# Two-layer fp32 encoder: the modulation sums are copied out one filling step ahead of their transposes, and GpSimd sums all squares of the first layer's last norm for two ranges

## The chip, the cores and the metric

The kernel runs on one core of a Trainium2 chip. The metric is the device time of one launch in microseconds (us). The kernel before takes 1818.6 us, the median of three runs (1816.88, 1818.6 and 1819.7 us).

## The reference

A small encoder of two layers with d = 1024 works on two sequences, a prompt of 256 tokens and a sample of 512 tokens, in fp32. Each sequence has a condition vector c, from which each layer makes six modulation vectors:

```python
for l in range(DEPTH):
    mod = jax.nn.silu(c) @ adaln_w[l] + adaln_b[l]
    sh1, sc1, g1, sh2, sc2, g2 = [t[:, None, :] for t in jnp.split(mod, 6, axis=-1)]
    h = rmsnorm(x, norm_g[l, 0]) * (1 + sc1) + sh1
    y = mlstm_mixer(...) if l % 2 == 0 else swa_mixer(...)
    x = x + g1 * y
    h = rmsnorm(x, norm_g[l, 1]) * (1 + sc2) + sh2
    x = x + g2 * conv_ffn(h, ...)
return rmsnorm(x, final_g)
```

Layer 0 mixes with an mLSTM of four heads, run forward and backward, whose output is multiplied by a sigmoid gate of its own and projected. Layer 1 mixes with attention in a sliding window. Both have a feed-forward part with a convolution of width 3 over the tokens (d_ff = 2816). The norm is `y = xf * lax.rsqrt(jnp.mean(xf * xf, axis=-1, keepdims=True) + EPS)`, then times its gain.

## The kernel before

**Layout.** Activations lie transposed: 128 channels on the partitions, tokens along the free axis, eight chunks of channels for the 1024. There are 768 tokens: the sample's 512 come first in the order of work, in two ranges of 256, and the prompt's 256 are the third range (`RANGES`). A product in fp32 is made of three matmuls: each operand is split into a high and a low half (`whi`, `wlo` for weights, `zh`, `zl` for normed activations), and high times high, high times low and low times high are summed. The split of a weight block of 128x1024 is a cast on ScalarE (ACT, L278) and a subtraction on VectorE (DVE, L279), after its DMA from HBM through SyncE's queue (SP).

**Order of the work.** The code is written as one stream per engine with tiles in rotating buffers; a scheduler then decides the order of instructions on each engine from the order of the code and its own estimate of when things are ready. On the chip each engine runs its own stream in that order and waits at an instruction until its inputs and its buffer are there, so nothing behind a waiting instruction passes it.

**Filling steps.** The modulation of layer 0 for the groups 2 to 5 (a group is 1024 columns of adaln_w: g1, sh2, sc2, g2) is made inside the mLSTM, in pieces. `adaln_g` (from L472) is a generator: it fetches two blocks of adaln_w (`raw`), yields, multiplies them with silu(c) on TensorE (PE; rows `ps<-raw,silc`, four matmuls of 32 output rows for a block, into four column groups of one bank `ps`), and so on through eight blocks. At the end the sums in `ps` are copied into `sb` (one half by DVE at L499, the other by ACT at L500), PE transposes the two halves (L503), and DVE adds the bias into `mod` (L508). Four such generators are chained as `self.fillp` (L1761). Heads 1 to 3 of the mLSTM take 11 steps each from the chain: after a piece of q and k (L790), after every second tile of v (L805), and two at each sequence (L872). What is left of the chain after the heads and the output gate is run at once by `first` (L1764).

```python
self.fillp = chain(*(self.adaln_g(0, grp) for grp in range(2, 6)))
self.fill = self.adaln_v(1, pool)
act = self.mlstm(pool, gates, xt)
for _ in chain(self.fillp, self.fill):
    pass
```

A second generator, `adaln_v`, makes layer 1's modulation on DVE (L540, rows `ada<-raw,silc,ada`) and sums over partitions with ones on PE; its steps (`self.fill`) are taken between those of `fillp`.

**The end of the mLSTM.** After head 3 come the output gate's products (`ps<-zh,whi` and so on, 128x256 and 128x512): ACT takes the sigmoid (`sg`, L916), POOL (GpSimd) multiplies it with the mLSTM's output (L917), and ACT and DVE split the result (`slab<-sg`, L278 and L279). Then the output projection starts, with `ps<-slab,whi` 128x384 as its first row.

**The norms.** `Norm` (L91) sums the squares of the eight channel chunks of a range. ACT squares a chunk (L112). With `on_pe` = n, all chunks but the last n are added up on POOL (L121), one after another, and the sum and the n last squares are each multiplied by a constant matrix (`inv`) on PE for each 128 tokens, summed over the channels (`pa<-inv,nt`, 128x2). DVE adds epsilon (L161), POOL raises to the power -1/2 (L162), and PE spreads the factor `nr` over the partitions (`pa<-kct,nr`). DVE multiplies it with x (L583), ACT adds the shift and rounds into `zh` (L585), and DVE makes `zl` (L586). In `down` the last pass of a layer's feed-forward part makes the tiles of x (`pa` or `ps<-slab,whi` and `wlo`, added to x by DVE at L624) and squares them at once for the norm that follows; `keep` is given in layer 0 alone. In layer 0 these norms have `on_pe` = 2: five adds on POOL and six products with inv in each range. The first window products of layer 1 (`ps<-zh,whi`, `ps<-zl,whi`, `ps<-zh,wlo`) follow the second range's zh and zl while the tiles of the next range are still made.

Of the kernel before, what the change touches and what calls it, by code (L numbers as in the profile page):

```python
# [24 lines left out]
RANGES = ((256, 512, 0), (512, 768, 0), PROMPT)  # L25
# [55 lines left out]
def col(t):  # L81

    return t + (GAP if t >= 256 else 0)
# [101 lines left out]
class Net:  # L185
# [290 lines left out]
    def adaln_g(self, l, grp):  # L476

        nc = self.nc
        fetch = lambda k: self.raw(
            self.io["adaln_w"][l, k * P : (k + 1) * P, grp * 1024 : (grp + 1) * 1024]  # L480
        )
        part = [fetch(0), fetch(1)]
        yield
        ps = self.ps()
        for k in range(0, KC, 2):

            with self.tc.manual_schedule(engines={mybir.EngineType.PE}):
                for z in (1, 0):
                    for g in range(4):
                        self.mm(  # L490
                            ps[32 * g : 32 * g + 32, :256], self.silc[:, k + z, :],
                            part[z][:, g * 256 : (g + 1) * 256], k + 1 - z == 0, k + 1 - z == KC - 1,
                        )
            if k < KC - 2:
                part = [fetch(k + 2), fetch(k + 3)]
                yield
                yield
        sb = self.stg.tile([P, 2, P], F32, tag="raw", name=self.nm("sb"), bufs=5)
        nc.vector.tensor_copy(sb[:, 0], ps[:, :P])  # L499
        nc.scalar.copy(sb[:, 1], ps[:, P : 2 * P])  # L500
        pt = self.ps()[:, : 2 * P]
        for b in range(2):
            nc.tensor.transpose(pt[:, b * P : (b + 1) * P], sb[:, b], self.ident)  # L503
        src = pt.rearrange("p (b g s) -> p g b s", b=2, g=4)
        dst = self.mod[l][:, grp * 8 : (grp + 1) * 8, :].rearrange("p (g b) s -> p g b s", g=4)
        ab = self.cst(AB + 48 * l + 8 * grp, 8).rearrange("p (g b) -> p g b", g=4)
        for s in range(2):
            nc.vector.tensor_tensor(dst[:, :, :, s], src[:, :, :, s], ab, ALU.add)  # L508
        i = {1: 0, 4: 1}.get(grp)
        if i is not None:  # L510
            for s in range(2):
                nc.vector.scalar_tensor_tensor(
                    self.gain[l][i][:, :, s], self.mod[l][:, grp * 8 : (grp + 1) * 8, s], 1.0,
                    self.cst(NG + (2 * l + i) * 8, 8), ALU.add, ALU.mult,
                )
        yield
# [1077 lines left out]
    def ffn(self, l, xt, pool, last_tile, apply, keep=None):  # L1594
# [68 lines left out]
        def down(p, g):  # L1663
            ws = (w for _, w in self.halves(u0 + 3 * p + 2))
            chunk = lambda w, i: [t[:, 512 * i : 512 * (i + 1)] for t in w]

            def tile(w, c, rng, more=False):
                s0, s1, _ = rng
                o = (self.ps() if more and (c % 2 or c == KC - 2 and p == NPART - 1 and rng is RANGES[-1]) else self.pa())[:, : s1 - s0]
                cs = slice(c % 4 * P, (c % 4 + 1) * P)  # L1670
                for i in range(2):
                    wh, wl = chunk(w, i)
                    gh, gl = (g[:, z, i, col(s0) : col(s0) + s1 - s0] for z in range(2))
                    self.mm(o, wh[:, cs], gh, i == 0, False)
                    self.mm(o, wh[:, cs], gl, False, False)
                    self.mm(o, wl[:, cs], gh, False, i == 1)
                return self.resid(xt, o, l, 40, c, rng)

            if p < NPART - 1:
                for h, w in enumerate(ws):  # L1680
                    for rng in SAMPLE, PROMPT:
                        for c in range(4 * h, 4 * h + 4):
                            tile(w, c, rng, p == NPART - 2)
                return
            ws = list(ws)
            for rng in RANGES:
                final = keep is None and rng is RANGES[-1]
                norm = Norm(
                    self, xt, rng, apply, 4 if final else 2, final,
                    None if keep is not None or final else nc.vector, 0.0 if keep is None or rng is RANGES[-1] else 1.3,  # L1690
                    4.5 if keep is None and rng is RANGES[1] else 2.0,
                )
                for c in range(KC):
                    done = tile(ws[c // 4], c, rng, keep is None or rng is not RANGES[-1])
                    norm.square(c)
                    if final and c >= KC - 2:
                        self.ends.append(done.ins)
                    if final and c == KC - 1:
                        norm.sums = norm.sums[2:] + norm.sums[:2]
                        self.counted = norm.begin(3)  # L1700
                    self.tick(0.65)
                if keep is not None:
                    self.save_x(xt, keep, rng)
                self.start(rng, norm.stages())

        prev = None
        for p in range(NPART):
            g = up(p)
            if prev is not None:
                down(*prev)  # L1710
            prev = (p, g)
        down(*prev)


# [177 lines left out]
```

## Time and profile before

| | |
|---|---|
| median of three runs | 1818.6 us (1816.88 to 1819.7) |
| the profiled run | 1819.56 us, its span 1817.0 us |
| granted TensorE clock in it, mean | 0.996 of full speed |
| PE / DVE / ACT / POOL busy, share of the span | 98% / 76% / 49% / 26% |
| DMA, share of 16 engines through the main queue | 31.0% |
| products with inv of 128x2, PE at 1008.50 us | six in 1.25 us |

The profile is one execution. A row of its timeline has the start in us from the span's start, the duration in us, engine, line, operation, output<-inputs by the program's names, the shape, and xN for N instructions in a row; a matmul stands in these rows as two records in some shapes. What stands in brackets is how long the engine had been idle before and what released it. PE's rows overlap, since matmuls are pipelined: the time that a matmul costs is read from start to start.

### The profile page before, as it was taken

What the parts mean: (1) busy time and instruction counts of PE and PEld (TensorE: products, weight loads), DVE (VectorE), ACT (ScalarE), POOL (GpSimd) and SP (SyncE); (2) the same over time, 40 slices, a digit from 0 to 9 for tenths busy, and PEclk for the clock granted to TensorE, in tenths of its full rate; (3) what the DMA queues carried; (4) which work ended last, traced back from release to release, by engine and by line L of the source; (5) the groups of instructions that cost most, each with busy time, mean ns of one, the idle gap of its engine ahead of it and who ended that gap; (6) DMA issues with size and microseconds to landing.
All of it is one profiled execution on the core that took longest, in us unless ns stands there. A gap on an engine that the chain in (4) does not pass through costs nothing.

```text
span 1817.0 us, 28981 instructions
## 1 busy us (share of the span) xinstructions
PE 1782.3 (98%) x11282; PEld 1649.1 (91%) x11282; DVE 1386.8 (76%) x2148; ACT 890.0 (49%) x1798; POOL 478.4 (26%) x391
## 2 busy tenths in 40 slices
PE   7999999999999999999999999999999999999998
PEld 4988888889998999999999999889989999999997
DVE  4876676786799778777877867767998778777777
ACT  4553433434465444444444657665564444444443
POOL 3000000031024333333331313320234333333322
PEclk9999999999999999999999999999999999999998
DMA  9334565656212122222222331234122222222212
GB/s 337 115 119 147 176 205 192 205 165 216 87 49 81 59 70 70 70 69 67 64 69 95 106 92 42 61 95 133 47 81 70 70 70 70 70 70 71 70 36 70
DMA packets 64788, 184.01 MB, mean 101 GB/s; under 512 B 6199, under 2 KB 24759, under 8 KB 64652
## 3 DMA queue, kind: packets, MB, share of 16 engines
q1 hardware_dynamic: 64076, 181.65, 31.0%
q8 instruction: 88, 1.44, 0.3%
q10 hardware_dynamic: 576, 0.52, 0.1%
q14 instruction: 48, 0.39, 0.1%
HBM read 175.72 MB, written 6.43 MB: 100 GB/s over the span
## 4 chain that ended last, share of the span: by engine, by line
PE 84%; DVE 6%; DMA 4%; ACT 3%; issue 1%; POOL 1%; SPq 0%; POOLq 0%; ACTq 0%; DVEq 0%
PE ps L272 26%; PE pa L272 24%; PE ps L1372 10%; PE ps L1375 10%; PE ps L1373 10%; DMA raw<-in_w_dram 2%; PE pa L1211 1%; DMA raw<-in_adaln_w_dram 1%; ACT whi L278 1%; DVE wlo L279 1%; DVE ada L540 1%; DMA slab<-in_adaln_w_dram 1%; PE pa L1372 0%; PE pa L1373 0%; DVE wlo L1497 0%
## 5 line engine op out<-in xcount | busy, mean ns | idle before, releaser
L278 ACT CAST whi<-raw 128x1024 fp32r<-128x1024 f32 (+1 forms) x231 | 241.0, 1045 | 338.8 <-PE pa L272 143.9
L279 DVE TENSOR_TENSOR wlo<-raw,whi 128x1024 fp32r<-128x1024 f32 (+1 forms) x231 | 314.5, 1363 | 115.0 <-ACT whi L278 112.8
L272 PE MATMUL pa<-slab,whi 128*128 128x256 f32 (+1 forms) x1324 | 316.2, 334 | 0.0
L272 PEld LDWEIGHTS pa<-slab,whi 128*128 128x128 f32 x1324 | 229.0, 188 | 21.6 <-DVE slab L624 0.4
L624 DVE SCALAR_TENSOR_TENSOR slab<-pa,mod,slab 128x256 f32<-128x256 f32 (+1 forms) x331 | 192.3, 599 | 62.6 <-PE pa L272 62.4
L272 PE MATMUL pa<-slab,wlo 128*128 128x256 f32 (+1 forms) x662 | 211.8, 332 | 0.0
L272 PE MATMUL ps<-zh,whi 128*128 128x256 f32 (+1 forms) x560 | 187.4, 336 | 0.3 <-ACT zh L970 0.3
L272 PE MATMUL ps<-zl,whi 128*128 128x256 f32 (+1 forms) x560 | 183.6, 330 | 0.5 <-DVE zl L586 0.5
L272 PE MATMUL ps<-zh,wlo 128*128 128x256 f32 (+1 forms) x560 | 180.7, 328 | 0.0
L1372 PE MATMUL ps<-zh,whi 128*128 128x384 f32 x504 | 172.5, 342 | 3.8 <-ACT nt L1443 1.9
L1373 PE MATMUL ps<-zl,whi 128*128 128x384 f32 x504 | 169.9, 337 | 1.6 <-DVE zl L1329 1.6
L1375 PE MATMUL ps<-zh,wlo 128*128 128x384 f32 x504 | 169.2, 336 | 0.0
L272 PE MATMUL ps<-slab,whi 128*128 128x384 f32 (+2 forms) x660 | 164.4, 332 | 0.9 <-DVE slab L279 0.5
L1408 POOL TENSOR_TENSOR raw<-raw,raw 128x512 f32<-128x512 f32 x40 | 53.7, 1344 | 318.3 <-DVE wlo L279 245.8
L272 PEld LDWEIGHTS pa<-slab,wlo 128*128 128x128 f32 x662 | 124.5, 188 | 13.2 <-DVE wlo L279 0.4
L1624 POOL TENSOR_TENSOR slab<-slab 128x772 f32<-128x772 f32 x44 | 86.5, 1967 | 169.6 <-DVE slab L1612 157.6
L1611 DVE SCALAR_TENSOR_TENSOR slab<-slab,cstt,slab 128x771 f32<-128x771 f32 x88 | 106.3, 1210 | 26.6 <-ACT slab L1609 26.4
L540 DVE SCALAR_TENSOR_TENSOR ada<-raw,silc,ada 128x1024 f32<-128x1024 f32 x84 | 111.0, 1355 | 20.0 <-DMA raw<-in_adaln_w_dram 20.0
L272 PEld LDWEIGHTS ps<-slab,whi 128*128 128x128 f32 x660 | 115.9, 188 | 3.4 <-ACT whi L278 0.9
L272 PEld LDWEIGHTS ps<-zl,whi 128*128 128x128 f32 x560 | 106.0, 190 | 13.6 <-issue 4.6
L272 PEld LDWEIGHTS ps<-zh,whi 128*128 128x128 f32 x560 | 106.2, 190 | 12.3 <-issue 3.5
L272 PEld LDWEIGHTS ps<-zh,wlo 128*128 128x128 f32 x560 | 105.0, 190 | 9.1
(307 smaller groups left out, 4301.4 us busy)
## 6 DMA issues: line engine op xcount, KB each, us to landing
raw<-in_w_dram SPq DMA_DIRECT2D x208, 512.0 KB, 3.7
raw<-in_adaln_w_dram SPq DMA_DIRECT2D x84, 512.0 KB, 4.5
slab<-in_x_dram SPq DMA_DIRECT2D x12, 512.0 KB, 7.6
slab<-in_adaln_w_dram SPq DMA_DIRECT2D x11, 512.0 KB, 10.3
slab<-mrows SPq DMA_DIRECT2D x8, 384.0 KB, 5.0
xs<-slab SPq DMA_DIRECT2D x6, 512.0 KB, 3.2
bt<-brow SPq DMA_DIRECT2D x16, 192.0 KB, 3.2
slab<-xs SPq DMA_DIRECT2D x6, 512.0 KB, 7.1
```

Source lines behind the costliest of these rows:

```text
L272: self.nc.tensor.matmul(out, lhsT, rhs, start=start, stop=stop)
L278: nc.scalar.copy(hi, src)
L279: return nc.vector.tensor_tensor(lo, src, hi.bitcast(F32), ALU.subtract)
L540: stt(acc[:, s], row, w, acc[:, s], ALU.mult, ALU.add)
L624: return self.nc.vector.scalar_tensor_tensor(x, o, self.mod[l][:, gc + c, q : q + 1], x, ALU.mult, ALU.add)
L1211: nc.tensor.transpose(pp[:, ks], b.t[:, e, ks], self.ident)
L1372: mm(o, wh[:, k], hi[k], start=start and k == 0, stop=False, skip_group_check=True)
L1373: mm(o, wh[:, k], lo[k], start=False, stop=False, skip_group_check=True)
L1375: mm(o, wl[:, k], hi[k], start=False, stop=k == 3, skip_group_check=True)
L1408: tt(q[0], q[2], q[0], ALU.subtract)
L1611: stt(y[:, 1:], u[:, :-1], w(0), y[:, 1:], ALU.mult, ALU.add)
L1624: nc.gpsimd.tensor_tensor(y, y, yrow[:, j], ALU.mult)
```

## The change

```diff
@@ adaln_g
         sb = self.stg.tile([P, 2, P], F32, tag="raw", name=self.nm("sb"), bufs=5)
         nc.vector.tensor_copy(sb[:, 0], ps[:, :P])
         nc.scalar.copy(sb[:, 1], ps[:, P : 2 * P])
+        yield
         pt = self.ps()[:, : 2 * P]
         for b in range(2):
             nc.tensor.transpose(pt[:, b * P : (b + 1) * P], sb[:, b], self.ident)
@@ down
                 norm = Norm(
-                    self, xt, rng, apply, 4 if final else 2, final,
+                    self, xt, rng, apply, 4 if final else 0 if keep is not None and rng is not RANGES[-1] else 2, final,
                     None if keep is not None or final else nc.vector, 0.0 if keep is None or rng is RANGES[-1] else 1.3,
                     4.5 if keep is None and rng is RANGES[1] else 2.0,
                 )
```

The first part makes a group nine steps instead of eight: the copies out of `ps` end a step, and the transposes begin the next one. Four groups have 36 steps instead of 32, and the heads take 33. The second part sets `on_pe` to 0 in layer 0's last norm for the first two ranges, so POOL makes seven adds in each and PE two products with inv. Lines behind L500 have numbers one higher in the changed file. The orders below are those of the built programs.

PE in head 2, at the end of one group's sums (ps_2104) and its transposes (kct is the identity, sb the copied sums), before:

```order
L272 MATMUL ps_2662<-wlo_2628,zh 128x256
L272 MATMUL ps_2104<-raw_2434,silc 32x256 x3
L272 MATMUL ps_2104<-raw_2432,silc 32x256 x4
L503 MATMUL ps_2703<-kct,sb_2700 128x128
L272 MATMUL ps_2708<-whi_2621,zh 128x256
L272 MATMUL ps_2708<-whi_2621,zl 128x256
```

and after, where the same group's sums end well ahead (the products with slab that follow them are q times k) and its transposes stand behind a whole product of v:

```order
L272 MATMUL ps_2104<-raw_2332,silc 32x256
L272 MATMUL ps_2104<-raw_2330,silc 32x256 x4
L272 MATMUL pa_2498<-slab_2178,slab_2334 128x512 x6
...
L272 MATMUL ps_2792<-wlo_2628,zh 128x256
L504 MATMUL ps_2819<-kct,sb_2758 128x128 x2
L272 MATMUL pa_2862<-slab_2616,PT_2512 128x258 x2
```

The transposes moved from right behind the last sums to more than a hundred rows behind them.

ACT at the end of the output gate (sg is the sigmoid, whi_4580 and the next two are the projection's first weight blocks), before:

```order
L916 ACTIVATE sg_4519<-ps_4477 128x512
L278 CAST whi_4580<-raw_4578 128x1024
L278 CAST whi_4586<-raw_4584 128x1024
L278 CAST slab_3936<-sg_4519 128x512
L278 CAST whi_4649<-raw_4647 128x1024
L916 ACTIVATE sg_4549<-ps_4524 128x256
L278 CAST slab_3936<-sg_4549 128x256
```

and after:

```order
L917 ACTIVATE sg_4500<-ps_4458 128x512
L278 CAST slab_3917<-sg_4500 128x512
L917 ACTIVATE sg_4530<-ps_4505 128x256
L500 COPY sb_4546<-ps_3691 128x128
L278 CAST slab_3917<-sg_4530 128x256
L278 CAST whi_4580<-raw_4578 128x1024
L278 CAST whi_4586<-raw_4584 128x1024
```

The copy of the last group's sums has come in, and the casts of the projection's weights stand behind the gate's last cast. On PE at the same place the last gate product was followed by the projection; now there stand between them the last group's last sums and its transposes:

```order
L272 MATMUL ps_4505<-zh,wlo_4455 128x256
L272 MATMUL ps_3691<-raw_3852,silc 32x256 x3
L504 MATMUL ps_4549<-kct,sb_4546 128x128 x2
L272 MATMUL ps_4562<-slab_3914,whi_4580 128x384 x2
L272 MATMUL ps_4562<-slab_3914,wlo_4581 128x384
```

POOL at the last norm of layer 0 (nt_9579 is the first range's sum, nt_9662 or nt_9664 the second's), before, from the first range's last add on:

```order
L121 TENSOR_TENSOR nt_9579<-nt_9579,nt_9630 128x256
L121 TENSOR_TENSOR nt_9662<-nt_9662,nt_9671 128x256
L162 TENSOR_TENSOR nr_9681<-nr_9681,mhalf 128x2
L121 TENSOR_TENSOR nt_9662<-nt_9662,nt_9692 128x256
L121 TENSOR_TENSOR nt_9662<-nt_9662,nt_9702 128x256
```

and after:

```order
L121 TENSOR_TENSOR nt_9579<-nt_9579,nt_9630 128x256
L121 TENSOR_TENSOR nt_9664<-nt_9664,nt_9673 128x256
L121 TENSOR_TENSOR nt_9579<-nt_9579,nt_9641 128x256
L121 TENSOR_TENSOR nt_9579<-nt_9579,nt_9651 128x256
L162 TENSOR_TENSOR nr_9679<-nr_9679,mhalf 128x2
L121 TENSOR_TENSOR nt_9664<-nt_9664,nt_9690 128x256
```

The two added adds of the first range stand behind the first add of the second.

## The prediction

> **What bounds the kernel now.** I read the page's head, its busy table and its chain of waits first, then PE's own rows in the two stretches that the change touches, then the rows of the engines that PE waits for there.
>
> ```profile
> span 1817.0 us, 28981 instructions
> PE 1782.3 (98%) x11282; PEld 1649.1 (91%) x11282; DVE 1386.8 (76%) x2148; ACT 890.0 (49%) x1798; POOL 478.4 (26%) x391
> PE 84%; DVE 6%; DMA 4%; ACT 3%; issue 1%; POOL 1%; SPq 0%; POOLq 0%; ACTq 0%; DVEq 0%
> ```
>
> TensorE (PE) is busy for 1782.3 of 1817.0 us and carries 84% of the chain that ended last; all idle time of PE together is 34.7 us. So a change of order can pay only where PE stands still, it costs wherever it makes PE stand still, and a matmul taken away pays its own length. Every term below is therefore a length of PE's time. The profiled run took 1819.56 us, 2.56 us more than its span and 0.96 us above the median, 1818.6 us, so I add the sum to the profiled run and take 0.96 us off at the end. A measurement of this kernel can tell about 0.2%, 3.6 us, from no change.
>
> **The wait that the extra step aims at.** The view of the transposes' line, and PE, DVE and ACT around the one of the four groups that waits:
>
> ```profile
> L503 PE MATMUL ps<-kct,sb x8: 270/272/328, 186.5 to 357.6; 128*128 128x128 f32 x8
>   DVE sb L499: 3.8, 2
> ...
> 250.81 1.06 PE L272 MATMUL ps<-raw,silc 128*32 128x256 f32 x14
> 253.55 0.33 PE L503 MATMUL ps<-kct,sb 128*128 128x128 f32 x1 [1.68 <-DVE sb L499]
> ...
> 252.47 0.83 DVE L279 TENSOR_TENSOR PT<-E,PT 128x640 fp32r<-128x640 f32 x1
> 253.21 0.28 DVE L499 COPY sb<-ps 128x128 f32<-128x128 f32 x1
> ```
>
> The line waited twice in all; the 3.8 us add up a wait of the weight load and one of the matmul for the same event, since only one row on PE shows idle time, 1.68 us at 253.55. There the sums ended at 251.87 (250.81 + 1.06), but DVE reached the copy at 253.21, behind a chain that ends in the 0.83 us row. The other three groups' transposes show no wait. In the changed program the first group's transposes stand where they stood, and the three others follow their copies by dozens of matmuls or more, except the last. So the term is **-1.7 us**, once. What is late next: behind the transposes PE has 48 products of whi, wlo with zh, zl that ask nothing of the copy, and DVE's rows there keep their order but for the copy, so I see nothing that takes the wait's place.
>
> **The sums are cut up more often.** The extra step also shifts every later filling step: the sum matmuls (raw, silc) fall into other gaps. The rows give the price of a cut:
>
> ```profile
> 189.40 0.62 PE L272 MATMUL ps<-raw,silc 128*32 128x256 f32 x2
> 189.94 0.50 PE L272 MATMUL pa<-slab,PT 128*128 128x258 f32 x2
> 190.38 1.06 PE L272 MATMUL ps<-raw,silc 128*32 128x256 f32 x14
> 191.37 0.50 PE L272 MATMUL ps<-zh,whi 128*128 128x512 f32 x1
> ...
> 203.96 1.07 PE L272 MATMUL ps<-raw,silc 128*32 128x256 f32 x16
> 204.96 0.50 PE L272 MATMUL ps<-zh,whi 128*128 128x512 f32 x1
> ```
>
> Eight sum matmuls (16 records) in one run hold PE from 203.96 to 204.96, 1.00 us. Cut into 1 and 7 they hold it from 189.40 to 189.94 and from 190.38 to 191.37, 0.54 + 0.99 = 1.53 us. A cut costs 0.53 us, because a short run still takes half a microsecond. From the row after the first group on, the sums of the groups stand in 13 unbroken runs before and in 16 now (the same 88 matmuls): 3 x 0.53 = **+1.6 us**. Bounds: 0, if a new short run lies in a wait anyway, to 2.1 for a fourth cut (the products of ada with ones are cut once too).
>
> **The last group falls behind the gate products.** 33 steps are taken inside the heads; four groups had 32 and have 36 now, so three steps are left over. They run after the last gate product, where the program now has three sum matmuls, two copies, two transposes, and only then the output projection. These are the rows of before at that place:
>
> ```profile
> 428.51 0.28 PE L272 MATMUL ps<-zh,wlo 128*128 128x256 f32 x1
> 428.63 0.51 PE L272 MATMUL ps<-slab,whi 128*128 128x384 f32 x2
> 428.99 0.34 PE L272 MATMUL ps<-slab,wlo 128*128 128x384 f32 x1
> ...
> 426.08 1.99 ACT L278 CAST whi<-raw 128x1024 fp32r<-128x1024 f32 x2
> 429.67 0.38 ACT L916 ACTIVATE sg<-ps 128x256 f32<-128x256 f32 x1
> 431.00 0.41 ACT L278 CAST slab<-sg 128x256 fp32r<-128x256 f32 x1 [0.96 <-POOL sg L917]
> ...
> 427.16 2.62 DVE L279 TENSOR_TENSOR wlo<-raw,whi 128x1024 fp32r<-128x1024 f32 x2 [0.95 <-ACT whi L278]
> ...
> 430.12 0.85 POOL L917 TENSOR_TENSOR sg<-sg,slab 128x256 f32<-128x256 f32 x1 [2.56 <-ACT sg L916]
> ```
>
> PE went from the last gate product at 428.51 to the projection at 428.63 without a gap, because ACT had cast the first two weight blocks (426.08 to 428.07) and DVE had made the first low half (from 427.16, about 1.3 us) beside the gate products. In the changed order these casts stand on ACT behind the last sigmoid, the copy of the sums, and the cast of the last gate; the low halves stand on DVE behind the same things. Let E be the end of the last gate product. The sigmoid (0.38) ends at about E + 0.55. The gate's multiplication on POOL (0.85) ends at about E + 1.5, and ACT, which has copied the sums by then (the three sums take 0.54, the copy some 0.25), waits for it: cast of the gate (0.41) to E + 1.95, first weight cast (half of 1.99) to E + 3.0. Only then can the projection start. Its third matmul needs the low half, 1.3 us later on DVE, at E + 4.3; before, it stood at 428.99, E + 0.36. That is 3.9 us later, of which 0.9 us is PE's own moved work (three sums 0.54, two transposes 0.33), counted already. **+3.1 us**. Queued behind the two casts are the third one and the low halves of the next blocks; a weight block feeds 12 matmuls of 0.17 us, 2 us, against 1.3 us a block on DVE, so it does not grow. Bounds: 2.0, if PE's first two products and the casts overlap better than I walk them, to 4.0 for the gap with no deduction.
>
> **The norm at the boundary of the layers.** POOL adds all eight squares in the first two ranges: one add more per square and range, 2 x 2 adds; PE's products with inv fall from 6 to 2 in each range. Rows of the first range:
>
> ```profile
> 1003.68 4.70 POOL L121 TENSOR_TENSOR nt<-nt,nt 128x256 f32<-128x256 f32 x6 [8.60 <-ACT nt L112]
> ...
> 1008.50 1.40 PE L272 MATMUL pa<-inv,nt 128*128 128x2 f32 x12
> 1009.75 0.48 PE L272 MATMUL pa<-slab,whi 128*128 128x256 f32 x2
> 1010.17 0.71 POOL L162 TENSOR_TENSOR nr<-nr,mhalf 128x2 f32<-128x2 f32 x1 [1.79 <-DVE nr L161]
> 1011.26 0.60 PE L272 MATMUL pa<-kct,nr 128*128 128x128 f32 x4
> ```
>
> An add takes 4.70 / 6 = 0.78 us, and POOL's six fill 1003.68 to 1008.38: five of this range, and already one of the next. In the new order the two extra adds stand behind that one, so the last ends at 1003.68 + 8 x 0.78 = 1009.95. PE comes to inv at 1008.50 as before and now waits 1.5 us. Then two products for six: they took 1.25 us (1008.50 to 1009.75), 0.21 each, so 0.83 is saved. Net **+0.7 us**. The factor itself stays covered: between inv and the products with nr (1011.26) stand three tiles of PE, 1.5 us, and the rows from inv to the end of POOL's power are 1.1 us.
>
> The second range:
>
> ```profile
> 1013.92 0.61 DVE L586 SCALAR_TENSOR_TENSOR zl<-nt,mod,zh 128x256 fp32r<-128x256 f32 x1
> 1014.46 0.47 DVE L624 SCALAR_TENSOR_TENSOR slab<-pa,mod,slab 128x256 f32<-128x256 f32 x1
> 1014.85 0.47 DVE L583 SCALAR_TENSOR_TENSOR nt<-slab,gain,pa 128x256 f32<-128x256 f32 x1
> 1015.24 0.47 DVE L586 SCALAR_TENSOR_TENSOR zl<-nt,mod,zh 128x256 fp32r<-128x256 f32 x1
> ...
> 1014.59 0.39 PE L272 MATMUL ps<-zl,whi 128*128 128x256 f32 x1 [0.50 <-DVE zl L586]
> 1017.85 0.95 PE L272 MATMUL pa<-inv,nt 128*128 128x2 f32 x8
> 1021.96 0.71 PE L272 MATMUL pa<-kct,nr 128*128 128x128 f32 x4 [0.32 <-POOL nr L162]
> ...
> 1013.52 1.61 POOL L121 TENSOR_TENSOR nt<-nt,nt 128x256 f32<-128x256 f32 x2
> ```
>
> Before, PE put tiles of the down product and pieces of inv between the window products that use one zl after the other. In the new order inv waits until all adds are made, the tiles go behind it, and the products of the first four zl follow one another. DVE makes rows of this kind every 0.39 us (1014.46, 1014.85, 1015.24), and from one zl to the next there are three, two and three rows now: 1.17, 0.78, 1.17 us, against three products of 0.12 us. PE so waits 0.8 + 0.4 + 0.8 = 2.0 us. POOL's last add ends by my walk just before PE comes to inv. Back come four products at 0.2 (the eight records at 1017.85 are four, 0.81 us to the next) and the 0.32 us at 1021.96, whose factor now has four tiles ahead of it. Net 2.0 - 0.8 - 0.3 = **+0.9 us**. Bounds of both ranges together: -2.0, if the adds are always ready and DVE runs ahead (2 x 0.8 and 0.3 saved), to +4.5, if POOL's two adds also come late in the second range (2 x 0.78 more, plus the same again as slack in my walk).
>
> Beside POOL's two adds at 1013.52 the zl row at 1013.92 took 0.61 us; the next one, at 1015.24 with POOL idle, took 0.47. The two extra adds of the second range lie beside two zl rows: 0.14 each, within the bounds. [...]
>
> **The sum**: -1.7 + 1.6 + 3.1 + 0.7 + 0.9 = +4.6 us. 1819.56 + 4.6 = 1824.2, less 0.96: **1823 us**, 0.25% slower. The rest of the first stretch (heads one to three) is reshuffled too; I walked PE's waits there and found none that is surely new, so it stands at zero with bounds of -1 and +4.
>
> **The rivals.**
> (a) *The tail stays covered* (ends not slower). If the first casts of the projection were ready at E after all, for instance because the moved work and the gate's cast take less than the gate products ahead of them, the +3.1 goes: +1.5 us, 1820 us. It decides from a tail below 2.1 us. Against it speaks ACT's order: a cast can't pass the gate's cast, which waits for POOL (0.96 us already before). 0.25.
> (b) *VectorE's reshuffle in head one.* The ada products (1.25 us each) now stand one pair ahead of the rows that release PE's banks after the first outputs, and wait for their own DMA. If the release comes 2 to 4 us late, PE stands: 1826 us. For it: DVE is 76% busy. Against it: PE has over 2 us of products before it needs the first such bank. 0.15.
> (c) *Only the gains arrive*: the wait (-1.7) and the twelve, now four, inv products (-1.6) pay, and the cuts, the tail and the waits on POOL hide: 1815 us or less. It needs several of the above to be wrong. 0.08.
> [...] 0.05. [...]
> My forecast has the remaining 0.47.
>
> **How the numbers follow.** The range reaches from a little below rival (a), 1817, to 1828, above (b). Below 1815.0 (faster by over 0.2%) lies (c): 0.08. Within 0.2%, 1815.0 to 1822.2, lie (a) and a part of the forecast where tail and norm come out at their low ends: 0.37. Above 1822.2: 0.55.
>
> **What would show it.** In the profile after: the row of the third group's transposes without idle time; short runs of raw, silc of about 0.5 us, three more of them; at some 430 us a first projection product that waits about 2 us for ACT's cast and another that waits 1.3 us for DVE's wlo; near 1010 us an inv row that waits about 1.5 us for POOL, and three waits for zl behind it. If PE shows no wait at the tail, the largest term is wrong; if new waits for DVE or for banks appear between 190 and 400 us, the zero for the reshuffle is.

## The result and the profile after

The changed kernel takes 1835.3 us, the median of five runs (1831.7 to 1835.4), against 1818.6 us: 1.0086 times as long, with a 95% interval of 1.0075 to 1.0098. It is 16.6 us slower. I had forecast 4.4 us more, in a range from 1817 to 1828.

The page's head, busy table and chain of waits of the changed kernel's profiled run (1835.25 us):

```profile
span 1833.5 us, 28941 instructions
PE 1791.0 (98%) x11266; PEld 1651.6 (90%) x11266; DVE 1391.3 (76%) x2148; ACT 890.5 (49%) x1798; POOL 482.5 (26%) x395
PE 83%; DVE 8%; DMA 3%; ACT 3%; issue 2%; POOL 1%; SPq 0%; POOLq 0%; DVEq 0%; ACTq 0%
```

PE has 8 products with inv fewer to make, yet it is busy for 8.7 us longer: the same work must have taken longer somewhere. PE's share of the span is 98% as before. To find the places I compare the start of one and the same PE instruction in both traces (before, after, and how much later than at the place above):

| place on PE | before | after | added here |
|---|---|---|---|
| products of 128x512 behind the first waits, code that the change does not touch | 117.98 | 120.71 | +2.7 |
| last gate product (heads 1 to 3 lie in between) | 428.51 | 435.24 | +4.0 |
| third matmul of the projection (the tail) | 428.99 | 439.44 | +3.7 |
| first tile behind the first range's inv | 1009.75 | 1020.94 | +0.7 |
| `pa<-zh,whi` x3 (the second range's zl lie in between) | 1040.42 | 1055.29 | +3.7 |
| `ps<-whi,zh` behind the third range's zl | 1055.42 | 1074.12 | +3.8 |
| end of the span | 1816.97 | 1833.46 | -2.2 |

The tail, on PE and on ACT, reads as forecast:

```profile
435.45 0.63 PE L272 MATMUL ps<-raw,silc 128*32 128x256 f32 x6
436.57 0.53 PE L504 MATMUL ps<-kct,sb 128*128 128x128 f32 x2 [0.49 <-DVE sb L499]
438.18 0.63 PE L272 MATMUL ps<-slab,whi 128*128 128x384 f32 x2 [1.07 <-ACT whi L278]
439.44 0.45 PE L272 MATMUL ps<-slab,wlo 128*128 128x384 f32 x1 [0.64 <-DVE wlo L279]
...
436.77 0.41 ACT L278 CAST slab<-sg 128x256 fp32r<-128x256 f32 x1
437.08 2.94 ACT L278 CAST whi<-raw 128x1024 fp32r<-128x1024 f32 x3
```

With E at 435.36 (the last gate product and 0.12), the projection starts at E + 2.8 and its third matmul at E + 4.1; the forecast had 3.0 and 4.3. The three weight casts stand behind the gate's cast.

The norm at the layers' boundary, on PE and DVE:

```profile
1020.48 0.61 PE L272 MATMUL pa<-inv,nt 128*128 128x2 f32 x4 [1.26 <-POOL nt L121]
1025.72 0.38 PE L272 MATMUL ps<-zl,whi 128*128 128x256 f32 x1 [0.44 <-DVE zl L587]
1026.90 0.39 PE L272 MATMUL ps<-zl,whi 128*128 128x256 f32 x1 [0.56 <-DVE zl L587]
1027.69 0.39 PE L272 MATMUL ps<-zl,whi 128*128 128x256 f32 x1 [0.16 <-DVE zl L587]
1029.37 0.58 PE L272 MATMUL ps<-zl,whi 128*128 128x256 f32 x1 [1.05 <-DVE zl L587]
1029.75 0.42 PE L272 MATMUL ps<-zh,wlo 128*128 128x256 f32 x1
1029.96 0.41 PE L272 MATMUL ps<-zh,whi 128*128 128x256 f32 x1
1059.10 0.41 PE L272 MATMUL pa<-zl,whi 128*128 128x256 f32 x1 [2.17 <-DVE zl L587]
...
1028.34 0.97 DVE L587 SCALAR_TENSOR_TENSOR zl<-nt,mod,zh 128x256 fp32r<-128x256 f32 x1
1055.73 2.80 DVE L1074 TENSOR_TENSOR slab<-ps,slab 64x512 fp32r<-64x512 f32 x4
1058.56 2.46 DVE L587 SCALAR_TENSOR_TENSOR zl<-nt,mod,zh 128x256 fp32r<-128x256 f32 x6
```

The wait for POOL and the three added waits for zl are there. What no step of the forecast had is in the last columns of two rows: from 1029.75 to 1029.96 is 0.21 us for a product of 128x256 that costs 0.12 elsewhere. The windows show why. Their columns are PE's busy time, the granted clock, and the DMA's share and rate:

```profile
118.00:120.00 2.00, 2.00 (x10) 0.50 0.04 8
1026.00:1028.00 2.00, 1.28 (x8) 1.00 0.71 238
1028.00:1030.00 2.00, 0.95 (x6) 0.65 0.01 5
1030.00:1032.00 2.00, 2.00 (x11) 0.50 0.00 0
1032.00:1034.00 2.00, 2.00 (x11) 0.50 0.00 0
1034.00:1036.00 2.00, 2.00 (x14) 0.65 0.38 129
1060.00:1062.00 2.00, 2.00 (x11) 0.50 0.11 36
```

Between 40 and 1800 us the granted clock falls to one half three times: near 119, behind the second range's waits and behind the third range's wait. At 1028 to 1036 the missing shares (0.35 + 0.5 + 0.5 + 0.35) make 6.8 us at one half; the same sum gives 3.4 us at 116 to 122 and at 1058 to 1064. A 256-wide product loses 0.09 of 0.21 us there, so 6.8 us of work at one half cost some 2.9 us and 3.4 us cost 1.5. In the second range PE still stood for 0.8 of the 6.8 us, since the clock falls at 1028.59 and the last wait ends at 1029.37; that leaves some 2.6 us. In the profile of before the clock is 1.00 from 40 to 1800 us.

The second range is then: waits 0.56 + 0.16 + 1.05 = 1.8, half clock 2.6, less four products (0.8) and the old wait (0.3), 3.3 of the 3.7 in the table. A wait here also cost some 0.2 us beyond the idle time that its row shows: the products at 1026.06 and 1026.90, with the wait of 0.56 between them, hold PE until 1027.12, 1.06 us, where two such products in a row take 0.24. That is about the rest. The third range: 2.17 + 1.5 = 3.7 of 3.8.

### The profile page after: what moved, and what is told of

It reads as the page before. It is cut to its first block, busy times and chain, and to the rows that moved or that the text cites. A ratio compares the mean times of both kernels' runs of the same rounds, so it can differ in the third digit from the quotient of the medians.

```text
span 1833.5 us, 28941 instructions
## 1 busy us (share of the span) xinstructions
PE 1791.0 (98%) x11266; PEld 1651.6 (90%) x11266; DVE 1391.3 (76%) x2148; ACT 890.5 (49%) x1798; POOL 482.5 (26%) x395
## 4 chain that ended last, share of the span: by engine, by line
PE 83%; DVE 8%; DMA 3%; ACT 3%; issue 2%; POOL 1%; SPq 0%; POOLq 0%; DVEq 0%; ACTq 0%
PE ps L272 25%; PE pa L272 24%; PE ps L1373 10%; PE ps L1376 10%; PE ps L1374 10%; DMA raw<-in_w_dram 2%; PE pa L1212 1%; DVE ada L541 1%; DMA raw<-in_adaln_w_dram 1%; DVE wlo L279 1%; ACT whi L278 1%; DVE slab L625 1%; DMA slab<-in_adaln_w_dram 0%; PE pa L1374 0%; PE pa L1373 0%
```

## The experiments

Two theories had to be told apart. **A**: the loss is PE's new waits, made worse where they lie so close together that PE's clock is halved behind them. **Rivals**: the clock is chance and has nothing to do with the change; or copies apart from their transposes, or adds on POOL, cost by themselves. In the expectations theory C is the first of these rivals; what B means is said in each part where it first stands. All medians below stand against before's on the same chip, 1818.1 to 1819.3 us.

### The two parts, and the two ranges

```diff
 e1    nc.scalar.copy(sb[:, 1], ps[:, P : 2 * P]); yield          # norm as before
 e2    ... 0 if keep is not None and rng is not RANGES[-1] else 2  # no yield
 e3    ... 0 if keep is not None and rng is RANGES[0] else 2       # no yield
 e4    ... 0 if keep is not None and rng is RANGES[1] else 2       # no yield
```

> Only the extra filling step. Theory A (the changed kernel's loss is the sum of new waits of PE, made worse where PE's granted clock falls to half after waits that come close together): about 1825 to 1827 us, +7 us, of which 3.7 us between the last gate product and the projection's third matmul and about 4 us between 200 and 430 us, with the norm's place at full clock. Theory B (the recorded sum was right for this part and the rest of the loss is the norm's or chance): about 1821.6 us, +3.0.

1828.0 us, ratio 1.0054 (1.0042 to 1.0066): the rise, 9 us, is above what even theory A asked for. In the profiled run, the slowest of the five (1830.9 us), the clock falls behind the tail too:

```profile
438.00:440.00 2.00, 1.36 (x5) 0.53 0.97 318
440.00:442.00 2.00, 2.00 (x8) 0.50 0.94 303
...
444.00:446.00 2.00, 2.00 (x10) 0.76 1.03 399
```

The order of instructions at the tail is that of the change, and its waits are the same (1.06 and 0.64 us), but in the changed kernel's profile the clock stayed at 1.00 here. So behind the same waits the clock was halved in one execution and not in the other; how often it falls here in runs that were not profiled isn't shown. Since order and waits are the same, the pair gives the price of the clock by itself: the 24 matmuls from the projection's third one on take 4.31 us, start to start, in the change and 7.09 us in e1, 2.8 us more.

> Only the norm: on_pe 0 in the first two ranges. Theory A: +8 us, about 1826, with the clock at one half for some 6 us behind the zl waits of the second range. Theory C (the half clock is chance of one execution and does not belong to the change): +1.6 to +4 us, 1820 to 1823, the waits for zl and for POOL alone, clock 1.00 there.

1825.0 us, ratio 1.0030 (1.0018 to 1.0042): +5.9 us, between the two theories' numbers, but the half clock of theory A is there:

```profile
1022.00:1024.00 2.00, 1.88 (x9) 0.52 0.00 0
1024.00:1026.00 2.00, 2.00 (x11) 0.50 0.00 0
...
1028.00:1030.00 2.00, 2.00 (x16) 0.77 0.96 288
```

The wait of 2.17 us in the third range is missing here: with the norm's change alone DVE's order has one zl ahead of the first subtractions of L1073. By the table above that is 3.8 us less than in the whole change.

> The norm's change in the first range alone. One wait of PE for POOL of 1.3 to 1.5 us at the products with inv, four products saved. Theories A and C alike: +0.6 to +0.7 us, within the spread of the runs, and the clock stays at 1.00, since one wait of that length is not enough.

1819.7 us, ratio 1.0001 (0.9993 to 1.0010). PE waits 1.29 us for POOL once, and the clock stays at 1.00 behind it, as both theories had it.

> The norm's change in the second range alone. Theory A: the four waits for zl come within 4 us and the clock falls to one half behind them: +6 to +7.5 us. Theory C: +1 to +3 us, clock 1.00.

1824.8 us, ratio 1.0036 (1.0024 to 1.0049). PE waits 0.56, 0.17 and 0.56 us more for zl, and the clock falls behind them:

```profile
1018.00:1020.00 2.00, 1.44 (x8) 0.75 0.00 0
1020.00:1022.00 2.00, 2.00 (x11) 0.50 0.00 0
...
1024.00:1026.00 2.00, 2.00 (x12) 0.55 0.53 180
```

So the second range carries the norm's loss. This kernel also has the third range's late zl, with its wait of 2.18 us at 1049 and the clock at one half behind it; it, too, has both pairs of L1073 ahead of that zl.

### The extra step without the tail

```diff
 e5   + yield;  self.step(self.fillp, (3 - q) if h else 0)          # 36 steps
 e6   nc.scalar.copy(...); yield from [None] * (grp == 3)           # 33 steps, none left over
 e9   + yield; ahead of the output gate's products:
      +        for _ in self.fillp:
      +            pass
```

> The extra filling step, with 36 steps taken in the heads instead of 33 (three at the first sequence of a head rather than two), so that the last group ends inside head 3. The norm is as before. Theory A (the loss of the extra step is the tail and the half clock behind it, the cuts and new waits in the heads): the projection follows the gate without a gap and at full clock as before, the wait of 1.7 us is gone, and the time is 1817 to 1820, against 1828.0 with 33 steps. Rival B (copies and transposes apart cost by themselves, wherever they stand): 1823 or more.

1819.9 us, ratio 1.0005 (0.9996 to 1.0014): theory A. No row at the projection has idle time, the clock stays at 1.00 there, no transpose waits. The sums stand in 17 runs, four more than before, at 0.53 each 2.1 us, and one batch of ada products is cut in two (1.0 us, see below), against the 1.7 us of waiting saved: that the time is not shorter than before is what these terms give.

> The extra filling step only for the one group whose transposes waited (33 steps in all, so none is left over). The norm is as before. Theory A: the wait of 1.7 us goes and no tail comes; 1817 to 1820 if the later groups' sums are not cut more. Rival B: 1822 or more, as a third of the loss of the extra step.

1819.9 us, ratio 1.0006 (0.9998 to 1.0015). Again the wait at the transposes is gone; a wait of 1.30 us for the last sigmoid stands ahead of the projection in its place, and the clock holds.

> The extra filling step alone with 33 steps in the heads, as in the change, but the three steps left over are taken right after head 3, ahead of the output gate's products, not behind them. The cuts and waits in the heads up to there stay nearly as they are. Theory A: the projection starts without a gap at full clock; of the 9 us of the extra step some 3.7 us (the tail's delay) and up to 3.4 us (half clock behind it) go: 1820 to 1822. Rival B (the heads' cuts and waits make the loss, the tail little): 1825 or more.

1823.9 us, ratio 1.0028 (1.0019 to 1.0037): 4.1 us better than with the left-over steps behind the gate, but not the 1820 to 1822 expected. The projection starts without a gap. The profile has a new wait instead, for a load of the sums' weights:

```profile
352.22 1.90 PE L272 MATMUL ps<-raw,silc 128*32 128x256 f32 x16 [3.31 <-DMA raw<-in_adaln_w_dram]
...
352.00:354.00 2.00, 1.78 (x16) 0.58 0.87 348
354.00:356.00 2.00, 2.00 (x14) 0.57 0.82 233
```

The half clock comes behind it once more, for 3.4 us, and this profile has another 3.4 us of it at 1322, behind waits for zl of 0.21, 0.20 and 0.96 us in code that the change doesn't touch. Waits for this load at about 352 us stand in five other profiles as well, with 0.56 to 2.24 us, in kernels whose code there is that of before; the time at which the transfer lands differs from one execution to the next. How much of the 4.6 us by which e9 is slower than before belongs to the heads' order and how much to this wait stays open.

### How much waiting halves the clock

```diff
 e7    ... 1 if keep is not None and rng is not RANGES[-1] else 2
 e8    first range only, on_pe 0; ahead of its last add:
       + [tensor_tensor(acc, acc, self.sums[-1], o) for o in (ALU.add, ALU.subtract)]
 e10   e8, and ahead of inv:
       + for _ in range(16):
       +     net.mm(pm[:, :P], self.x(KC - 1)[:, :P], net.ident, True, True)
```

> The norm's change by half: on_pe 1 in the first two ranges (six adds and four products with inv in each). Theory A: PE waits some 0.7 us for POOL in the first range (one add less than in the change), and in the second range the products of several zl again follow one another, since inv stands behind them in one piece; the half clock comes there, +4 to +6 us. Rival: the zl waits need all eight squares on POOL; then within 1 us of before.

1820.5 us, ratio 1.0010 (1.0001 to 1.0019): less than theory A expected. The products of the first three zl do follow one another (waits of 0.51, 0.56 and 0.17 us), and in the profiled run, one of the longer ones at 1821.3 us, the clock fell for nearly 7 us behind them. The runs reach from 1817.0 to 1824.0 us, and only one was profiled: how often the clock falls in the others isn't shown. Both expected sizes were off.

> A dose of waiting: the first range alone with all squares on POOL, and two more adds on POOL ahead of the last (the square is added and taken away again), so PE waits there once for about 1.3 + 1.6 = 2.8 us. If the clock follows the share of waiting within some 3.4 us (theory A), it falls to one half behind this wait, for 3.4 or 6.8 us: +2.2 us for the wait and +1.7 to +3.4 us for the clock, 1823 to 1825. If only waits that come in a row with short work between them do it (rival), the clock stays at 1.00 and the time is 1821.

1825.6 us, ratio 1.0037 (1.0027 to 1.0048). The wait is 2.86 us and the clock falls behind it, without any short work in between:

```profile
1014.40 0.61 PE L272 MATMUL pa<-inv,nt 128*128 128x2 f32 x4 [2.86 <-POOL nt L121]
...
1012.00:1014.00 2.00, 0.00 (x0) 1.00 0.00 1
1014.00:1016.00 2.00, 1.60 (x9) 0.74 0.00 0
1016.00:1018.00 2.00, 2.00 (x11) 0.50 0.10 25
```

The late zl of the third range is in this kernel too, so its time is not that of the one wait alone. Its wait is as long as in the change, but here the clock stays at 1.00 behind it:

```profile
1050.80 0.39 PE L272 MATMUL pa<-zl,whi 128*128 128x256 f32 x1 [2.17 <-DVE zl L586]
...
1052.00:1054.00 2.00, 2.00 (x19) 1.00 0.20 50
```

> The first range alone with all squares on POOL and two more adds ahead of the last, as in the longer wait, but PE makes 16 products of 128x128 with the identity, whose result nothing reads, ahead of the products with inv, about 1.7 us. POOL's sum comes as late as before and PE's idle time at inv shrinks from 2.9 to about 1.1 us. Theory A (the clock follows PE's idle share within some 3.4 us): the granted clock stays at 1.00 there and the time falls by 1.7 us or more against the longer wait without them, to 1822 to 1824. Rival (the half clock is chance or follows something else than PE's idling): the clock falls as often as before and the time is the same or longer, 1825 or more.

1823.3 us, ratio 1.0023 (1.0013 to 1.0033). The products took 3.73 us, not 1.7, and so filled the wait at inv altogether; the scheduler also moved tiles and later rows, and a wait of 1.61 us for nr came behind.

```profile
1010.08 3.73 PE L274 MATMUL pa<-kct,slab 128*128 128x128 f32 x32
1017.87 0.71 PE L274 MATMUL pa<-kct,nr 128*128 128x128 f32 x4 [1.61 <-POOL nr L164]
...
1014.00:1016.00 2.00, 2.00 (x20) 1.00 0.01 4
1016.00:1018.00 2.00, 0.39 (x4) 1.00 0.77 259
```

The clock stays at 1.00 and the time falls by 2.3 us, although PE does more work. That is theory A's side; since the order around it changed as well, and the third range's wait of 2.17 us is gone, the 2.3 us are not the clock's price alone.

### The order of the second range, mended

```diff
 e11   e4, and Norm(wait = 2.6 if rng is RANGES[1])  in place of 1.3
 e12   e11 with the 36 steps of e5
```

> The norm's change in the second range alone, with the norm's own waiting time ahead of inv raised from 1.3 to 2.6 for that range. POOL still makes seven adds and PE two products with inv, but in the order PE again has tiles of the down product between the products of the first zl and the next. Theory A (the loss of the second range is the zl products in a row, their waits, and the half clock behind them, not the adds on POOL): the three later zl waits go, the clock stays at 1.00 there, and the time is 1818 to 1820, against 1824.8 with 1.3. Rival (adds on POOL beside DVE's zl, or the late factor, cost by themselves): 1822 or more.

1817.4 us, ratio 0.9993 (0.9984 to 1.0001), 7.4 us less than with 1.3, for the same seven adds on POOL and the same two products with inv. One zl row waits for DVE, as in before, and the clock is 1.00 throughout:

```profile
1014.00:1016.00 2.00, 2.00 (x18) 1.00 0.36 121
1016.00:1018.00 2.00, 1.60 (x11) 1.00 0.00 0
1018.00:1020.00 2.00, 2.00 (x18) 1.00 0.78 262
```

The adds on POOL cost nothing that shows; the order that left PE nothing to do between two zl did, and with it the third range's late zl, which is gone too.

> Both parts without what cost: the extra filling step with 36 steps in the heads (no tail), and the second range's norm with all squares on POOL and the later inv; the first range as before. If nothing else is hidden, the sum of the two single results: 1817 to 1820, not to be told from before by more than 0.2%, since what is saved (1.7 us of waiting, 0.8 us of products with inv) is smaller than that. Rival (the parts disturb each other through the order, as the third range's late zl in the change): 1822 or more.

1819.4 us, ratio 1.0002 (0.9993 to 1.0011), the sum of its two parts within the spread. Neither e11 nor e12 beats before by more than the measurement can tell.

## Why the prediction was wrong, step by step

**The wait of 1.7 us** went, as said: in the heads no transpose waits after. The one that had waited is that of group 3, the second of the four.

**The cuts** (+1.6) are there, 16 runs for 13. I had put a cut of the products of ada with ones into the bound alone, at up to 0.5 us; it costs 1 us, for a half takes as long as the whole. Their rows after:

```profile
281.71 1.05 PE L272 MATMUL ps<-ada,ones 128*32 128x512 f32 x4
283.83 1.05 PE L272 MATMUL ps<-ada,ones 128*32 128x512 f32 x4
```

Before, all of them (x8, at 282.16) took 1.06 us.

**The tail** (+3.1, and 0.9 of moved work): right, 3.7 in all. The half clock behind it, there in e1's profile (6.8 us) and not in the change's, is what I had not counted.

**The first range** (+0.7): right, +0.7.

**The second range** (+0.9): the step that failed in size. Its waits were right in place and nearly in length (1.8 us for 2.0), but the step took them at their own length. The 6.8 us at half clock behind them, some 2.6 us, and the 0.2 us or so that each wait cost beside its length make +3.7 of it. e4 against e11 shows that it is the order with its waits: both have the same adds and products, and 7.4 us lie between them. About half of these is the third range's wait with the half clock behind it, 3.8 us in the change.

**"The rest of the first stretch stands at zero"**: the step that failed in place. The heads added 4.0 us where my terms give -1.7 + 1.6 - 0.9 = -1.0. New waits of PE there:

```profile
337.08 0.63 PE L272 MATMUL pa<-slab,PT 128*128 128x258 f32 x3 [0.46 <-ACT slab L278]
375.98 0.66 PE L761 MATMUL pa<-kct,slab 128*128 128x128 f32 x4 [0.72 <-ACT slab L896]
377.24 0.66 PE L761 MATMUL pa<-kct,slab 128*128 128x128 f32 x4 [0.36 <-ACT slab L896]
398.60 0.50 PE L272 MATMUL ps<-zh,whi 128*128 128x512 f32 x1 [0.94 <-ACT sg L917]
409.03 0.50 PE L272 MATMUL ps<-zh,wlo 128*128 128x512 f32 x1 [0.17 <-DVE wlo L279]
```

They make 2.7 us, and none comes from the ada products, which rival (b) had named: four wait for ACT, whose rows had moved as well, and one for a low half. Of the 5.0 us between the 4.0 and my -1.0, they and the cut of ada give 3.7; a wait of 0.59 us at 215, which before had, is gone; so some 2 us remain. The 0.2 us or so that each wait cost beside its length in the second range may be half of that; the rest I can't assign.

**What I left out.** I took the order behind the second range for unchanged. It was not: in the whole change DVE makes four subtractions (L1074) ahead of the third range's first zl, PE waits 2.17 us, and in this execution the clock halves again, 3.8 us. Also 2.7 us by 121 us and -2.2 us at the end come from code that the change doesn't touch. The first of these has the half clock too, and it is there at 118 in the profiles of e1, e2, e3, e5 and e8, not in those of before, e4, e6, e7 and e9 to e12: it comes and goes with the execution.

**POOL's adds beside DVE's zl**: one row is longer there, the zl at 1028.34, which took 0.97 us beside POOL's adds (1027.50 to 1029.04), 0.5 more than the usual 0.47; the zl at 1025.16 took 0.51 beside an add. It is a small part; in e11, 1817.4 us with the same seven adds, they cost nothing that shows. Rivals (a) and (c) did not come.

Taken together, I forecast 4.4 us for 16.6. The working had one price for idle time, its own length, and none for what PE's clock does afterwards: in the changed kernel's profile, between 40 and 1800 us, 13.6 us at half clock, some 5.6 us, of which the 1.5 us near 118 are not the change's.

## What to carry to other kernels

Where PE is the bound, add up the idle time that a new order gives within a few microseconds, not only each wait: waits of 0.2 to 1 us with three products between them cost their length here, 1.8 us, and then some 2.6 us in clock. Give PE other work between products that one engine feeds one by one, as the mended wait does. And when a step is inserted into a filling sequence, count the steps against the slots: three steps left over cost more than the wait that the step took away, and the order far behind the edit is to be read too.

## What the runs showed of the hardware

PE's granted clock fell to one half behind idle times of 1.2 to 3.3 us, in one to four waits, and stayed there for 3.4 or 6.8 us:

| idle time of PE just before | clock behind it |
|---|---|
| one wait of 1.26 to 1.29 us (the change's first range, e2, e3) | 1.00 |
| one wait of 1.68 us (before, at 253) | 1.00 |
| 1.05 and 0.27 us at 115 (e1) | one half, 3.4 us |
| 1.53 and 0.27 us at the same place (e10) | 1.00 |
| 0.49, 1.07 and 0.64 us within 4 us (the change's tail) | 1.00 in the change, one half in e1 with the same waits |
| 0.44 to 0.51, 0.56, 0.16 or 0.17 and 0.56 to 1.05 us within 4 us (the change, e2, e4; in e7 without the last) | one half, 6.8 us |
| one wait of 2.17 or 2.18 us (third range) | one half, 3.4 us, in the change and e4; 1.00 in e8 |
| one wait of 2.24 us (e4, at 351) | 1.00 |
| one wait of 2.86 us (e8) or 3.31 us (e9) | one half, 3.4 us |
| 2.86 us filled with products (e10) | 1.00 |

So the length of the idle time doesn't decide alone. The clock's records in the traces show what goes with it. In the changed kernel's profile the clock falls at 117.23, 1028.59 and 1059.31 us; the second stretch is this:

```profile
1028.59:1035.42 6.83, 6.05 (x28) 0.50 0.02 8
```

The falls are 911.36 and 30.72 us apart, 267 and 9 times 3.413 us, and in the profiles of before and of the change every stretch at one clock that lies inside the span is a whole number of 3.413 us: 525 in before, and 31, 1, 266, 2, 7, 1 and 223 in the change. So in these two executions the clock changed only on a grid of 3.413 us, and its falls stand behind stretches of the grid in which PE did little. My estimate of how much, from the start-to-start times in the same two profiles (0.12 us for 256 columns, 0.54 for three sums, 0.99 for seven): the stretches of the grid ahead of the three falls are filled by PE's work to 0.42 (from 113.82), 0.31 (from 1025.18) and 0.34 (from 1055.90); those from 434.67 in the change and from 250.56 in before are filled to 0.46 each, and the clock stays at 1.00 behind both. At the tail of e1 the 3.413 us ahead of the fall (434.70 to 438.12) begin just where the gate products end, filled to 0.36 by the same estimate, and half clock follows; in the change (434.67 to 438.08) the stretch still holds 0.7 us of them, and the clock stays at 1.00.

Equal waits were followed by half clock in one execution and not in another also near 116: 1.57 and 0.26 us in the change, 1.53 and 0.27 in e10. Nor did PE idle for 3.413 us on end ahead of a fall: 2.17 us in one wait, 2.2 us in four waits with work between them, or 1.3 us in two (e1, at 115) were enough here. Whether a fixed share of work decides, and which, these runs don't settle.
